# One streaming-encoder layer on one core: the scan's gating on VectorE, a 544-column convolution beside attention, head norm weights after the transposition

## The chip, the core and the metric

The kernel runs on one core of a Trainium2 chip. The core has TensorE (PE in the profile, its weight loads PEld), VectorE (DVE), ScalarE (ACT), GpSimd (POOL) and SyncE (SP, which issues DMAs). The metric is device time in microseconds for one execution, lower is better.

## The reference

One layer of a hybrid encoder on 1024 prompt frames and 64 frames of a running stream, which the kernel treats as T = 1088 columns, all in float32. Cut to what matters here:

```
proj = rmsnorm(x) @ w_in                       # -> z, xBC, dt, q, k, v, gate_ssm, gate_att
xbc  = silu(causal_dwconv(xBC, width 4))       # 3072 channels -> xs, B, C
y    = ssd_scan(xs, dt, B, C) + d * xs         # chunked state-space scan, 4 groups
y    = rmsnorm_per_group(y * silu(z)) * ssm_norm_w
o    = diff_attention(q, k, v, caches, lam)    # 8 heads, two softmaxes each
o    = rmsnorm(o, subln_w) * (1 - lambda_init)
x   += (sig(gate_ssm) * (y @ w_bs) + sig(gate_att) * (o @ w_ba)) @ w_out
x   += conv_ffn(rmsnorm(x))
```

The outputs are the new x, k and v, the scan's end states and the margins of both convolutions.

## The kernel before

Activations are held feature-major: 128 features on the partitions, frames along the columns. Projections multiply 128x128 weight blocks with 272-column quarters (QW) of the activations, two of which make a half (HT = 544). Each float32 product is made of three matmuls of split numbers (`hi`, `lo`; lines 170 to 172, from `product`). The program is written as generators that hand each other turns; from these the tile framework draws up a fixed order of instructions for each engine. A sequencer takes its engine's instructions strictly in that order and waits on semaphores, so an instruction that waits holds up all that stands behind it on its engine.

Two stages matter here.

**Attention** (about 560 to 1130 us of the span). Eight heads with nine query blocks ("units") each. A unit (`attend`) makes scores (L1111, L1112), a maximum (L1116 or L1120 on VectorE), exponentials (L1125 on ScalarE), the combination of both softmaxes (L1129 on VectorE), transpositions (L1140), their evacuation to `a_t` (L1145 ScalarE, L1147 VectorE), and the product with v (L1160), evacuated by ScalarE (L1161, L1162). Between these, `fill` puts in matmuls of a stream of remaining projections (`stream`), so that TensorE has work while the softmax runs: 24 tiles of the convolved projection (`conv_tiles`) and gate tiles (`gate_tiles`).

`conv_tiles` handles each quarter by itself. The previous quarter's last three columns are copied in front by POOL (L987, L989), ScalarE copies the matmuls' result into `pre` (L990), scales and biases it (L999), VectorE adds three shifted multiples (L1001), ScalarE takes the tanh (L1002), VectorE multiplies (L1003, which makes silu), and SyncE stores the result in `x_sc` (L1004). `pre` has two buffers and `cc` three.

`head_out` ends a head. From sums of squares it makes a factor per query (`rs`); nine VectorE instructions L1178 multiply each 128-query block by its factor and by the norm weights `wsub`, which lie along the columns. TensorE then transposes the blocks (L1186), ScalarE evacuates `hi` (L1189) and VectorE `lo` (L1190).

`head_tiles` issues a head's loads: queries, keys, values, and for the ninth unit cached keys and values (`cached`: `ch_t`, `cl_t`, `cv_t`). `cv_t` has two buffers; the cached loads are issued with the rest, but for head 0, whose loads wait in `later`.

**Scan** (about 1130 to 1500 us). Four groups, each with nine 128-frame chunks in three spans of up to 384 columns: 12 spans. `front` prepares a chunk: transpositions `tr` of the inputs (L1285), `cb` (L1287, L1288), the product `xx` on VectorE (L1294), exponentials (L1297), a causal mask by POOL (L1295) and a product on VectorE (L1298). `back` multiplies: `yi` (L1306), `ye` (L1312), sums on VectorE (L1313, L1314), and the new state from `stp` (L1318), with the old state's decay on POOL (L1323) and the sum on VectorE (L1325). At the end of a span, `gated` adds d * xs (L1332, VectorE), multiplies the 4 x 384 values by z (L1333, POOL), squares them (L1334, ScalarE) and adds up the four blocks in two steps (L1335, L1336, POOL). A chunk later `normed` sums over the partitions with TensorE (`gst`, L1340), makes a reciprocal root with ScalarE and L257, L258 on VectorE, and `scaled` multiplies (L1350) and splits (L1359). The same filler continues with the branch projections, whose weights are split by L155 and L156.

## Time and profile before

| what | value |
|---|---|
| median of 3 runs | 2420.58 us (2420.09 to 2423.67) |
| the profiled execution, its own time | 2425.83 us |
| its span, from the first to the last instruction | 2424.0 us |
| mean granted TensorE clock | 0.997 |
| VectorE busy, 560 to 1130 us | 445.2 us |
| VectorE busy, 1130 to 1500 us | 283.0 us |
| POOL busy, 1130 to 1500 us | 161.4 us |

The profile is one execution. Its page has the busy time of each engine, groups of instructions by source line (`L1333 POOL ... x12 | total, mean` with the idle time before them behind a second bar), and a list of waits. Names such as `y<-y,zin` are output and inputs. `x12` is a count. Windows give busy times for a stretch of the span, and the timeline the instructions in order of time.

### The profile page before, as it was taken

The numbers are of one execution on the slowest core, as the hardware profiler recorded it, in microseconds if no ns is written. First come the engines' busy times: TensorE is split into PE (matmuls) and PEld (weight loads), VectorE is DVE, ScalarE is ACT, GpSimd is POOL, SyncE is SP. The second block draws the span as 40 slices with busy tenths as digits, with TensorE's granted clock in tenths as the row PEclk, the third lists the DMA queues.
The fourth block names the chain that finished last, engine by engine and source line by source line (L and its number), as shares of the span: only waits on it lengthen the run. The fifth ranks groups of instructions, "written<-read, shape, count | busy, mean of one in ns | idle before, by whom it ended". The sixth has DMA issues, their size and how long they took to land.

```text
span 2424.0 us, 49267 instructions
## 1 busy us (share of the span) xinstructions
PE 2379.3 (98%) x18648; PEld 2306.1 (95%) x18648; DVE 1750.6 (72%) x3150; ACT 1217.8 (50%) x2695; POOL 731.4 (30%) x773
## 2 busy tenths in 40 slices
PE   8999999999999999999999999999999999999998
PEld 8999999999999999999888899999999999999998
DVE  4678987646868778884789776656866767677765
ACT  6454454325656666665666564334543334352442
POOL 0032433321101101111444442012254455444444
PEclk9999999999999999999999999999999999999999
DMA  7773868536555544435978955764124424367976
GB/s 240 274 245 129 265 218 303 168 104 205 163 157 153 164 143 135 143 104 180 352 264 267 344 190 186 210 208 142 66 82 157 143 98 160 127 199 200 245 182 105
DMA packets 295087, 449.78 MB, mean 186 GB/s; under 512 B 36601, under 2 KB 188290, under 8 KB 294850
## 3 DMA queue, kind: packets, MB, share of 16 engines
q1 hardware_dynamic: 265506, 387.00, 49.5%
q0 software_dynamic: 11040, 26.34, 5.5%
q10 hardware_dynamic: 18304, 33.30, 3.7%
q8 instruction: 146, 2.39, 0.4%
q14 instruction: 91, 0.75, 0.1%
HBM read 294.03 MB, written 152.50 MB: 184 GB/s over the span
## 4 chain that ended last, share of the span: by engine, by line
PE 44%; DVE 6%; DMA 3%; issue 2%; ACT 1%; POOL 1%; SPq 0%; POOLq 0%; DVEq 0%; ACTq 0%
PE mx L1617 13%; PE mx L1791 6%; PE mm L1617 5%; PE mm L170 2%; PE mm L172 2%; PE mm L171 2%; PE mx L170 2%; PE mm L1791 2%; PE mx L172 2%; PE mx L171 2%; PE yi L1306 1%; PE stp L1318 1%; PE ye L1312 1%; DMA b<-y_sc 1%; DMA m_sc<-b_g 1%
## 5 line engine op out<-in xcount | busy, mean ns | idle before, releaser
L170 PE MATMUL mm<-b,w_hi 128*128 128x272 f32 x1376 | 408.7, 297 | 0.0
L172 PE MATMUL mm<-b,w_lo 128*128 128x272 f32 x1376 | 404.2, 294 | 0.0
L171 PE MATMUL mm<-b,w_hi 128*128 128x272 f32 x1376 | 403.0, 293 | 0.0
L170 PEld LDWEIGHTS mm<-b,w_hi 128*128 128x128 f32 x1376 | 259.5, 189 | 5.7 <-issue 3.4
L171 PEld LDWEIGHTS mm<-b,w_hi 128*128 128x128 f32 x1376 | 259.6, 189 | 4.5 <-issue 3.1
L172 PEld LDWEIGHTS mm<-b,w_lo 128*128 128x128 f32 x1376 | 259.1, 188 | 3.6 <-issue 2.5
L1617 PE MATMUL mx<-m,w_hi 128*128 128x272 f32 x792 | 152.3, 290 | 1.2 <-ACT m L419 1.2
L420 DVE TENSOR_TENSOR wh<-w_f,wh 128x512 fp32r<-128x512 f32 (+1 forms) x156 | 151.6, 973 | 0.7 <-ACT wh L419 0.7
L1001 DVE SCALAR_TENSOR_TENSOR cc<-pre,par,cc 128x272 f32<-128x272 f32 (+1 forms) x288 | 139.6, 488 | 9.8 <-ACT cc L999 7.5
L1617 PE MATMUL mx<-n,wh 128*128 128x272 f32 x1056 | 141.6, 288 | 1.1 <-DVE u L1644 1.1
L1125 ACT ACTIVATE p_t<-sc,mx 128x512 f32<-128x512 f32 (+6 forms) x144 | 106.2, 740 | 67.5 <-DVE mx L1116 37.4
L1617 PEld LDWEIGHTS mx<-n,wh 128*128 128x128 f32 x1056 | 135.7, 188 | 1.3 <-DVE u L1644 1.3
L989 POOL COPY pre<-pre 128x3 f32<-128x3 f32 x72 | 27.7, 385 | 346.3 <-DVE cc L1003 182.1
L563 POOL TENSOR_TENSOR ws<-w_f 128x512 f32<-128x512 f32 (+1 forms) x51 | 69.3, 1360 | 198.2 <-DMA w_f<-in_win_dram 82.0
L1617 PEld LDWEIGHTS mx<-m,w_hi 128*128 128x128 f32 x792 | 124.4, 188 | 1.4 <-ACT m L419 1.4
L170 PE MATMUL mx<-b,w_hi 128*128 128x272 f32 x416 | 122.9, 296 | 2.0 <-ACT w_hi L155 1.5
L172 PE MATMUL mx<-b,w_lo 128*128 128x272 f32 x416 | 121.5, 294 | 0.0
L171 PE MATMUL mx<-b,w_hi 128*128 128x272 f32 x416 | 121.4, 292 | 0.0
L1617 PE MATMUL mx<-m,w_lo 128*128 128x272 f32 x396 | 114.2, 289 | 0.0
L1626 ACT ACTIVATE cc<-pre,par 128x544 f32<-128x544 f32 (+1 forms) x44 | 37.2, 846 | 146.2 <-DVE pre L1661 145.3
L156 DVE TENSOR_TENSOR w_lo<-w_f,w_hi 128x1024 fp32r<-128x1024 f32 (+1 forms) x74 | 92.8, 1256 | 22.5 <-ACT w_hi L155 22.1
L419 ACT CAST wh<-w_f 128x512 fp32r<-128x512 f32 (+1 forms) x156 | 95.2, 613 | 27.0 <-POOL w_f L569 8.3
(463 smaller groups left out, 7311.7 us busy)
## 6 DMA issues: line engine op xcount, KB each, us to landing
w_f<-in_win_dram SPq DMA_DIRECT2D x40, 512.0 KB, 4.3
w_f<-in_wup_dram SPq DMA_DIRECT2D x80, 256.0 KB, 2.9
w_f<-in_win_dram SPq DMA_DIRECT2D x76, 256.0 KB, 3.3
bc<-a_sc SPq DMA_DIRECT2D x32, 512.0 KB, 7.1
b<-y_sc SPq DMA_DIRECT2D x24, 544.0 KB, 8.1
h_sc<-hb SPq DMA_DIRECT2D x44, 272.0 KB, 2.1
ht<-h_sc SPq DMA_DIRECT2D x22, 544.0 KB, 4.7
t_sc<-ht SPq DMA_DIRECT2D x22, 544.0 KB, 2.9
```

The lines of the kernel that those rows point to most:

```text
L156: V.tensor_tensor(out=lo, in0=w, in1=hi, op=ALU.subtract)
L170: PE.matmul(ps, a_hi, b_hi, start=i == 0, stop=False)
L171: PE.matmul(ps, a_hi, b_lo, start=False, stop=False)
L172: PE.matmul(ps, a_lo, b_hi, start=False, stop=i == n - 1)
L419: S.copy(hi, src)
L420: V.tensor_tensor(out=lo, in0=src, in1=hi, op=ALU.subtract)
L563: G.tensor_tensor(out=s1, in0=q21, in1=q22, op=ALU.add)
L1001: V.scalar_tensor_tensor(cc[:, :m], pre[:, i : i + m], cw(i), cc[:, :m], ALU.mult, ALU.add)
L1125: act(p_t[:n, :nk], sc[c][:n, :nk], AF.Exp, bias=mx[:n, c : c + 1], accum_out=dst)
L1617: PE.matmul(ps, w[x][:, c], b[y][:, k], start=start and k == i == 0, stop=k == 3 and i == 2, skip_group_check=not start)
L1626: act(cc[:, :n], pre[h][:, :n], AF.Identity, bias=col(O_FB + f), scale=cw(0))
L1791: PE.matmul(ps, w[y][:, c], b[z][:, k], start=start and k == j == 0, stop=k == n - 1 and j == 2, skip_group_check=not start)
```

## The change

Three edits, which touch no projection.

1. In `gated`, the product with z and the two sums of squares go from POOL to VectorE.
2. In `conv_tiles`, the first quarter of each half is only copied into `pre`; the scaling, the three multiples, the tanh, the product and the store are made once per 544-column half. `cc` goes from three buffers to two of twice the width. `cv_t` goes to one buffer, and each head's cached loads are issued with its fourth unit, by way of `later`.
3. In `head_out`, one VectorE product multiplies eight blocks by their factors, and a second instruction the short ninth. The norm weights are applied per partition behind the transposition, in the two evacuations. The column `wcol` comes from one transposition of `wsub` (the tile `pw`) before the first head.

```diff
     def conv_tiles(tiles):
...
+                first = c % HT == 0
+                if first:
+                    pre = cv_pool.tile([P, HT + 6], F32, name="pre", tag="pre", bufs=2)
+                    if tail is None:
+                        G.memset(pre[:, 0:3], 0.0)
+                    else:
+                        G.tensor_copy(pre[:, 0:3], tail)
+                at = 3 + c % HT
                 n = min(w, TP - c)
-                pre = cv_pool.tile([P, QW + 6], F32, name="pre", tag="pre", bufs=2)
-                cc = cv_pool.tile([P, QW + 3], F32, name="cc", tag="cc", bufs=3)
...
+                S.copy(pre[:, at : at + n], ps[:, :n])
...
+                if first:
+                    return
+                c -= QW
+                n, m = min(HT, TP - c), HT
...
+                cc = cv_pool.tile([P, HT + 3], F32, name="cc", tag="cc", bufs=2)
...
-            cv_t = ak.tile([P, 4, P], F32, name="cv_t", tag="cv_t", bufs=2)
+            cv_t = ak.tile([P, 4, P], F32, name="cv_t", tag="cv_t")
...
-                cached()
+            later.append(cached)
...
-            for i in range(9):
-                n = min(P, T - i * P)
-                V.scalar_tensor_tensor(o_t[:n, i], o_t[:n, i], rs[:n, i : i + 1], wsub[:n], ALU.mult, ALU.mult)
+            V.tensor_tensor(out=o_t[:, :8], in0=o_t[:, :8], in1=rs[:, :8].unsqueeze(2).to_broadcast([P, 8, P]), op=ALU.mult)
+            V.tensor_scalar(o_t[:TS, 8], o_t[:TS, 8], rs[:TS, 8:9], None, ALU.mult)
...
-                S.copy(hi, pt[:, :w])
-                V.tensor_tensor(out=lo, in0=pt[:, :w], in1=hi, op=ALU.subtract)
+                act(hi, pt[:, :w], AF.Copy, scale=wcol)
+                V.scalar_tensor_tensor(lo, pt[:, :w], wcol, hi, ALU.mult, ALU.subtract)
...
+        pw = pa.tile([P, 512], F32, name="pw", tag="pt", bufs=2)
+        PE.transpose(pw[:, :P], wsub, ident)
+        S.copy(wcol, pw[:, 0:1])
...
+                if x == 3 and later:
+                    later.pop()()
...
         def gated(g, c, w, xs, zt, y):
...
-            G.tensor_tensor(out=y, in0=y, in1=zt, op=ALU.mult)
+            V.tensor_tensor(out=y, in0=y, in1=zt, op=ALU.mult)
             act(zt, y, AF.Square)
-            G.tensor_tensor(out=zt[:, 0:2], in0=zt[:, 0:2], in1=zt[:, 2:4], op=ALU.add)
-            G.tensor_tensor(out=zt[:, 0], in0=zt[:, 0], in1=zt[:, 1], op=ALU.add)
+            V.tensor_tensor(out=zt[:, 0:2], in0=zt[:, 0:2], in1=zt[:, 2:4], op=ALU.add)
+            V.tensor_tensor(out=zt[:, 0], in0=zt[:, 0], in1=zt[:, 1], op=ALU.add)
```

The framework orders the instructions anew, so both stages' orders differ in many places. Line numbers of the changed kernel are a little higher: L1294, L1298, L1313, L1314, L1325, L1332, L1350 become L1306, L1310, L1325, L1326, L1337, L1344, L1362 (12 more, POOL's L1295 and L1323 become L1307 and L1335), and L1001 and L1003 become L1009 and L1011.

VectorE at the end of the scan's first span, before:

```order
L1294 TENSOR_TENSOR xx<-tr,dtt 128x1024
L1332 SCALAR_TENSOR_TENSOR y<-in,par,y 128x384 x4
L1313 TENSOR_TENSOR y<-ye,e_14870 128x4x128
L1325 TENSOR_TENSOR state<-state,stp 128x512
L1314 TENSOR_TENSOR y<-y,yi 128x4x128
L1294 TENSOR_TENSOR xx<-tr,dtt 128x1024
L1313 TENSOR_TENSOR y<-ye,e_15022 128x4x128
L1325 TENSOR_TENSOR state<-state,stp 128x512
L1298 TENSOR_TENSOR bc<-bc,b_cb 128x1024
```

And now:

```order
L1306 TENSOR_TENSOR xx<-tr,dtt 128x1024
L1344 SCALAR_TENSOR_TENSOR y<-in,par,y 128x384 x4
L1325 TENSOR_TENSOR y<-ye,e_14338 128x4x128
L1337 TENSOR_TENSOR state<-state,stp 128x512
L1345 TENSOR_TENSOR y<-y,zin 128x1536
L1326 TENSOR_TENSOR y<-y,yi 128x4x128
L1306 TENSOR_TENSOR xx<-tr,dtt 128x1024
L1310 TENSOR_TENSOR bc<-bc,b_cb 128x1024
L1325 TENSOR_TENSOR y<-ye,e_14490 128x4x128
L1347 TENSOR_TENSOR zin<-zin 128x768
L1337 TENSOR_TENSOR state<-state,stp 128x512
L1310 TENSOR_TENSOR bc<-bc,b_cb 128x1024
```

The product L1345 stands in front of the next chunk's `y` and `xx`, and the first sum L1347, which waits for ScalarE's square of the product, in front of a state and a `bc`.

POOL at the same place, before:

```order
L1295 AFFINE_SELECT bc<-bc 128x1024
L1323 TENSOR_TENSOR state<-state,decs 128x512
L1333 TENSOR_TENSOR y<-y,zin 128x1536
L1323 TENSOR_TENSOR state<-state,decs 128x512
L1295 AFFINE_SELECT bc<-bc 128x1024
L1335 TENSOR_TENSOR zin<-zin 128x768
L1323 TENSOR_TENSOR state<-state,decs 128x512
L1336 TENSOR_TENSOR zin<-zin 128x384
```

And now:

```order
L1307 AFFINE_SELECT bc<-bc 128x1024
L1335 TENSOR_TENSOR state<-state,decs 128x512 x2
L1307 AFFINE_SELECT bc<-bc 128x1024
L1335 TENSOR_TENSOR state<-state,decs 128x512
L1307 AFFINE_SELECT bc<-bc 128x1024
```

Masks and decays follow each other with nothing between them.

VectorE early in the attention's third head, where `ors` are the factors of the second head, before:

```order
L1175 SCALAR_TENSOR_TENSOR ors<-on_9066,on_9065 128x9
L1178 SCALAR_TENSOR_TENSOR o_t<-o_t,ors,wsub 128x128 x4
L1127 RECIPROCAL sm<-sm 128x1
L1178 SCALAR_TENSOR_TENSOR o_t<-o_t,ors,wsub 128x128 x4
L1178 SCALAR_TENSOR_TENSOR o_t<-o_t,ors,wsub 64x128
L1119 MEMSET sc 64x2x64
L1128 SCALAR_TENSOR_TENSOR sm<-sm,nlam,s_8932 128x1
L1001 SCALAR_TENSOR_TENSOR cc<-pre,par,cc 128x272
L1120 TENSOR_REDUCE mx<-sc 128x2
L1129 SCALAR_TENSOR_TENSOR p_t<-p_t,sm 128x1024
L1001 SCALAR_TENSOR_TENSOR cc<-pre,par,cc 128x272
```

And now:

```order
L1009 SCALAR_TENSOR_TENSOR cc<-pre,par,cc 128x544
L1135 SCALAR_TENSOR_TENSOR sm<-sm,nlam,s_8796 128x1
L1182 SCALAR_TENSOR_TENSOR ors<-on_8922,on_8921 128x9
L1009 SCALAR_TENSOR_TENSOR cc<-pre,par,cc 128x544
L1136 SCALAR_TENSOR_TENSOR p_t<-p_t,sm 128x128
L1183 TENSOR_TENSOR o_t<-o_t,ors 128x1024
L1184 TENSOR_SCALAR o_t<-o_t,ors 64x128
L1154 COPY a_t<-pt 128x512
L1011 SCALAR_TENSOR_TENSOR cc<-pre,cc 128x544
```

Nine instructions on `o_t` have become two, and the wide steps of the convolution stand between the steps of a softmax (`sm`, `p_t`) as the narrow ones did.

More of the change, by code (lines that the diff above doesn't have):

```diff
@@ L978, in conv_tiles @@
         for f in tiles:
[L979 removed]
+            tail = pre = None
             def evac(ps, c, w):
[L982 to L995 removed]
+                nonlocal tail, pre
+                first = c % HT == 0
[6 more added lines that the diff above has]
+                at = 3 + c % HT
+                n = min(w, TP - c)
+                S.copy(pre[:, at : at + n], ps[:, :n])
+                if n < w:
+                    G.tensor_copy(pre[:, at + n : at + n + 3], par[:, O_CS + 3 * f : O_CS + 3 * f + 3])
+                    S.copy(pre[:, at + n + 3 : at + w + 3], ps[:, n:])
+                if first:
+                    return
+                c -= QW
+                n, m = min(HT, TP - c), HT
+                tail = pre[:, n : n + 3]
+                if n < HT:
+                    m = HT + 3
                     G.tensor_copy(conv_o[:, f, 0:3], tail)
[L997 removed]
+                    G.tensor_copy(conv_o[:, f, 3:6], pre[:, HT + 3 : HT + 6])
+                cc = cv_pool.tile([P, HT + 3], F32, name="cc", tag="cc", bufs=2)
                 cw = lambda i: col(O_CW + 4 * f + i)
@@ L1004, in evac @@
                 seen["stored"] = load(out=x_sc[P * f : P * (f + 1), c : c + n], in_=cc[:, :n])
-                if n < w:
-                    load(out=x_sc[P * f : P * (f + 1), c + n : c + w], in_=cc[:, n + 3 : m])
+                if n < HT:
+                    load(out=x_sc[P * f : P * (f + 1), c + n : c + HT], in_=cc[:, n + 3 : m])
             yield from project(win[B_X + f], evac)
@@ L1075, in head_tiles @@
                 values_of()
-                later.append(cached)
             else:
@@ L1202, in hybrid_layer @@
         wsub = at.tile([P, P], F32, name="wsub")
+        wcol = at.tile([P, 1], F32, name="wcol")
         V.tensor_scalar_mul(wsub, par[:, O_SUB : O_SUB + P], 1.0 - LAMBDA_INIT)
+        pw = pa.tile([P, 512], F32, name="pw", tag="pt", bufs=2)
+        PE.transpose(pw[:, :P], wsub, ident)
+        S.copy(wcol, pw[:, 0:1])
         for i in range(2):
```

12 lines of the change are left out of this document (removed).

## The prediction, as it was made before the run

> **What bounds the kernel now.** I read the page's engine totals first, then the two stages that the change touches, then TensorE's own waits there.
>
> ```profile
> PE 2379.3 (98%) x18648; PEld 2306.1 (95%) x18648; DVE 1750.6 (72%) x3150; ACT 1217.8 (50%) x2695; POOL 731.4 (30%) x773
> ```
>
> ```profile
> 560.00:1130.00 570.00, 567.24 (x4351) 543.81 (x4350) 445.24 (x1076) 359.03 (x974) 69.58 (x168) 1.00 0.49 149
> 1130.00:1500.00 370.00, 361.09 (x2912) 323.26 (x2911) 282.97 (x353) 223.86 (x536) 161.37 (x104) 1.00 0.81 268
> 1200.00:1300.00 100.00, 96.71 (x798) 86.77 (x798) 88.07 (x117) 63.52 (x150) 45.11 (x29) 1.00 0.82 273
> ```
>
> In the window rows the columns are length, busy time of PE, PEld, DVE, ACT and POOL, the clock, the DMA share and GB/s. TensorE is busy for 2379.3 of 2424.0 us and the change leaves its work alone except for one transposition. So the change can only move the time by TensorE's waits. In the attention stage (560 to 1130 us) TensorE sits idle for 570 - 567.2 = 2.8 us; in the scan (1130 to 1500) for 370 - 361.1 = 8.9 us. What ends those waits:
>
> ```profile
> PE yi L1306 <- DVE y L1314: 3.1, 2, 1.6
> PE tr L1285 <- DVE xx L1294: 2.3, 3, 1.4
> PE stp L1318 <- DVE state L1325: 1.0, 2, 0.8
> PE yi L1306 <- ACT y L1316: 0.7, 1, 0.7
> PE cb L1287 <- ACT b_cb L1290: 0.6, 1, 0.6
> PE mx L170 <- ACT grs L1343: 0.5, 1, 0.5
> PE gst L1340 <- POOL zin L1336: 0.5, 1, 0.5
> ```
>
> ```profile
> PE sc L1111 <- ACT p_t L1125: 1.1, 1, 1.1
> PE po L1160 <- ACT a_t L1145: 0.9, 2, 0.6
> PE po L1160 <- DVE a_t L1147: 0.5, 1, 0.5
> PE sc L1111 <- DMA kl<-k_st: 0.2, 1, 0.2
> ```
>
> Each row gives the waiter, whom it waited for, total us, times, longest. The scan's rows add up to 8.7 us, of which 6.4 end on VectorE; the attention's to 2.7 us. Those 11.4 us are about all there is to win: 0.5% of the kernel.
>
> **The change part by part: the scan.** Three operations per span (12 spans) leave POOL, which keeps the mask L1295 and the state's decay L1323:
>
> ```profile
> L1333 POOL TENSOR_TENSOR y<-y,zin 128x1536 f32<-128x1536 f32 (+1 forms) x12 | 41.7, 3476 | 35.8 <-DVE y L1332 35.8
> L1335 POOL TENSOR_TENSOR zin<-zin 128x768 f32<-128x768 f32 (+1 forms) x12 | 21.4, 1786 | 10.2 <-ACT zin L1334 10.1
> L1336 POOL TENSOR_TENSOR zin<-zin 128x384 f32<-128x384 f32 (+1 forms) x12 | 16.6, 1380 | 0.6
> L1295 POOL TENSOR_SCALAR_AFFINE_SELECT bc<-bc 128x1024 f32<-128x1024 f32 (+1 forms) x36 | 40.9, 1136 | 132.5 <-ACT e L1282 123.8 <-DMA b<-y_sc 5.4 <-DMA out_dram<-state 3.1
> ```
>
> The numbers behind the bar are total us and mean ns. POOL loses 41.7 + 21.4 + 16.6 = 79.7 us. VectorE takes them over; its prices come from operations of the same kind there (min/median/max ns):
>
> ```profile
> L1298 DVE TENSOR_TENSOR bc<-bc,b_cb x36: 672/1218/3589, 1143.2 to 1468.4; 128x1024 f32<-128x1024 f32 x32, 64x512 f32<-64x512 f32 x4
> L1359 DVE TENSOR_TENSOR y<-y,zin x12: 819/946/1658, 1200.9 to 1329.2; 128x768 fp32r<-128x768 f32 x8, 128x640 fp32r<-128x640 f32 x4
> L258 DVE SCALAR_TENSOR_TENSOR grs<-gn,gn x12: 493/928/1998, 1195.6 to 1498.4; 128x384 f32<-128x384 f32 x8, 128x320 f32<-128x320 f32 x4
> L1350 DVE SCALAR_TENSOR_TENSOR y<-y,par,grs x48: 537/607/3830, 1198.0 to 1500.4; 128x384 f32<-128x384 f32 x32, 128x320 f32<-128x320 f32 x16
> ```
>
> L1298 (1024 columns, two SBUF inputs) has its median at 1218; L1359 gives 946 for 768 columns (its median) and 819 for 640 (its minimum). That is (1218 - 946) / 256 = 1.06 ns a column. The product then takes 1218 + 512 x 1.06 = 1761 ns for 1536 columns and 1218 + 256 x 1.06 = 1489 for 1280; the first sum 946 and 819; the second 946 - 384 x 1.06 = 539 and 819 - 320 x 1.06 = 480. Eight wide and four narrow spans: 8 x 3.25 + 4 x 2.79 = 37.2 us more work on VectorE.
>
> But POOL's operations already cost VectorE time. Two places of the timeline (start, us, engine, line; waits in brackets):
>
> ```profile
> 1285.98 3.49 POOL L1333 TENSOR_TENSOR y<-y,zin 128x1536 f32<-128x1536 f32 x1 [3.08 <-DVE y L1332]
> 1286.43 3.59 DVE L1298 TENSOR_TENSOR bc<-bc,b_cb 64x512 f32<-64x512 f32 x1
> 1291.89 0.33 PE L1306 MATMUL yi<-bc,xx 128*64 128x128 f32 x2 [1.64 <-DVE y L1314]
> ...
> 1365.12 5.81 DVE L1350 SCALAR_TENSOR_TENSOR y<-y,par,grs 128x384 f32<-128x384 f32 x4
> 1365.28 3.78 POOL L1333 TENSOR_TENSOR y<-y,zin 128x1536 f32<-128x1536 f32 x1 [2.62 <-DVE y L1332]
> 1372.12 0.63 PE L1285 MATMUL tr<-con,in 128*64 128x128 f32 x4 [1.45 <-DVE xx L1294]
> ```
>
> A 64x512 product L1298, whose minimum is 672 ns, took 3.59 us and ended with POOL's product L1333, and TensorE's yi then waited 1.64 us. Four L1350, 4 x 607 ns by the median, took 5.81 us beside another L1333, and tr waited 1.45 us. So VectorE operations with two SBUF inputs stand still while POOL computes; L258's maximum of 1998 ns is such a hit too. How much that is over the scan, by the means:
>
> ```profile
> L1298 DVE TENSOR_TENSOR bc<-bc,b_cb 128x1024 f32<-128x1024 f32 x32 | 48.4, 1511 | 20.2 <-ACT bc L1297 11.5 <-ACT b_cb L1290 8.6
> L1350 DVE SCALAR_TENSOR_TENSOR y<-y,par,grs 128x384 f32<-128x384 f32 x32 | 25.0, 842 | 0.2
> ```
>
> L1298: 32 x (1511 - 1218) = 9.4 us; L1350: 32 x (842 - 607) = 7.5. The same difference over all two-input lines of the scan gives 38 us of stretch. By their share of POOL's busy time (79.7 of 161.4) the three leaving operations cause 19 us of it, by their share without the one-input mask (79.7 of 161.4 - 40.9) 25 us. VectorE's net load thus rises by 37.2 - 25 = 12 to 37.2 - 19 = 18 us on 283.0. I take 12, since the two quoted hits are both L1333's.
>
> [...]
>
> On TensorE's path: the two quoted waits go (1.64 + 1.45); gst no longer waits for POOL (0.5); stp's longest wait of 0.8 goes, if L258's stretch was its cause; of the other yi wait (3.1 - 1.64) I give half, 0.7. That is 5.1 us. Added: VectorE now passes 6.4 / 283 = 2.3% of its busy time on to TensorE, so 37.2 us of new work bring 0.9 us of new waits. Bounds of the scan: from 8.7 gained (all waits gone) to 12 lost (rival below). I take 5.1 - 0.9 = **4.2 us gained**.
>
> The new VectorE sums wait for ScalarE's square; queued behind them are xx, state and y, for which TensorE waits. In the order three to five VectorE operations stand between product and first sum, which cover about the square's time, except at the last span, where nothing else is left to hold up.
>
> **The attention.** Wide operations replace pairs of narrow ones; the FFN's convolution has them at 544 columns:
>
> ```profile
> L1001 DVE SCALAR_TENSOR_TENSOR cc<-pre,par,cc x288: 411/494/509, 566.9 to 1107.8; 128x272 f32<-128x272 f32 x120, 128x275 f32<-128x275 f32 x24
> L1003 DVE SCALAR_TENSOR_TENSOR cc<-pre,cc x96: 411/434/446, 570.4 to 1108.9; 128x272 f32<-128x272 f32 x72, 128x275 f32<-128x275 f32 x24
> L999 ACT ACTIVATE cc<-pre,par x96: 599/615/645, 566.2 to 1105.3; 128x272 f32<-128x272 f32 x72, 128x275 f32<-128x275 f32 x24
> L1002 ACT ACTIVATE pre<-cc x96: 414/431/468, 569.6 to 1108.5; 128x272 f32<-128x272 f32 x72, 128x275 f32<-128x275 f32 x24
> L1628 DVE SCALAR_TENSOR_TENSOR cc<-pre,par,cc x88: 773/786/1884, 1729.8 to 2188.9; 128x544 f32<-128x544 f32 x44, 128x546 f32<-128x546 f32 x44
> L1626 ACT ACTIVATE cc<-pre,par x44: 840/846/853, 1724.5 to 2179.6; 128x544 f32<-128x544 f32 x22, 128x546 f32<-128x546 f32 x22
> L1629 ACT ACTIVATE cc<-cc x44: 654/661/667, 1738.0 to 2190.7; 128x544 f32<-128x544 f32 x22, 128x546 f32<-128x546 f32 x22
> L1178 DVE SCALAR_TENSOR_TENSOR o_t<-o_t,ors,wsub x72: 332/343/373, 651.9 to 1126.2; 128x128 f32<-128x128 f32 x64, 64x128 f32<-64x128 f32 x8
> L1129 DVE SCALAR_TENSOR_TENSOR p_t<-p_t,sm x72: 326/809/1289, 580.6 to 1100.2; 128x512 f32<-128x512 f32 x8, 128x128 f32<-128x128 f32 x8, 128x384 f32<-128x384 f32 x8, 128x256 f32<-128x256 f32 x8
> ```
>
> VectorE: L1001 288 x 494 = 142 us becomes 144 x 786 = 113; L1003 96 x 434 = 41.7 becomes 48 operations between 661 and 786 ns (the lower is ScalarE's), say 725: 34.8. The heads' 72 x 343 = 24.7 us become eight 1024-column products of 1.22 us and eight small ones of about 0.34: 12.5. Together 48 us less on 445. ScalarE: L999 96 x 615 = 59.0 becomes 48 x 846 = 40.6; L1002 96 x 431 = 41.4 becomes 48 x 661 = 31.7: 28 us less on 359. The scale put into head_out's two evacuations counts as nothing: the same elements, 24 pairs of instructions; 0.1 us on each would be 5 us off TensorE's path. POOL's copies of the margin halve; POOL is idle for most of the stage. Stores of x_sc halve in number, which shortens SyncE's queue. The wait that changes is ScalarE's copy into pre: a buffer is now held through two quarters and a chain of 0.85 + 3 x 0.79 + 0.73 + 0.66 = 4.6 us. The 96 convolution quarters and 32 gate quarters of these 570 us come every 4.5 us, so the next use of a buffer is over 13 us after its chain begins. Were it late, the softmax's exponentials would queue behind the copy, and TensorE's scores behind them. The cached keys' loads go behind the fourth unit, and are first needed by the ninth; cv_t with one buffer is free by then, as its last reader is the ninth unit of the head before. Nothing of this is on TensorE's path: of its 2.7 us of waits, 2.5 end on ScalarE or VectorE. I take half of these, **1.3 us gained**; bounds 2.7 gained to 10.5 lost (rival below).
>
> The one new transposition stands ahead of the first score, where TensorE already waited 0.2 us for keys: 0 to 0.3 us, I take **0.1 lost**.
>
> Sum: -4.2 - 1.3 + 0.1 = -5.4. The profiled execution took 2425.8 us, 1.8 of it around the span of 2424.0; it would become 2420.4. It lies 5.2 us above the median of the runs, so the forecast there is 2420.6 - 5.4 = **2415.2 us**, 0.22% faster. About 0.2%, 4.8 us, is what a measurement of this kernel can tell from no change.
>
> **The rivals.**
> *More goes than I count.* All 11.4 us of waits vanish: 2409.2. For it: TensorE's waits sit mostly on ScalarE and VectorE, both relieved. Against it: several scan waits (ACT y, ACT b_cb, ACT grs) have nothing to do with POOL.
>
> *The gain is swallowed.* The waits removed come back behind VectorE's own 37 us, or the stretch stays because POOL's mask and decay now hit the new operations: what is left is the attention's 1.3 and little more, 2419. For it: of 38 us of stretch, 13 to 19 belong to operations that stay.
>
> *VectorE becomes the bound in the scan* (the other side). From 1200 to 1300 us VectorE is already busy 88.1 of 100. Twelve spans in 370 us make 3.2 in 100, at 3.1 us each 10.1: 98.2 of 100 if none of the stretch goes. Then 12.3 us, the net load, lie on TensorE's path and none of its waits go: 2420.6 + 12.3 = 2432.9. It decides once VectorE is busy for over some 95% of such a window. Against it: the quoted hits are long, and they go with L1333.
>
> *Wide convolutions hold up the attention.* A softmax step L1129 (72 units) that falls behind a wide operation waits up to 786 - 494 = 292 ns longer, on average half; if TensorE had no cover, 72 x 0.146 = 10.5 us: 2420.6 - 4.2 + 10.5 = 2426.9. Against it: TensorE's queue holds projection matmuls between the units, and waits only 2.8 us now. [...]
>
> **How the numbers follow.** Forecast 0.40, all waits gone 0.08 (both faster by over 0.2%: 0.48); swallowed 0.30 (within); VectorE bound 0.14, wide convolutions 0.08 (slower: 0.22). The range runs from 2407, a little under the second case, to 2430, which takes in the wide convolutions and most of the way to the bound VectorE; about 0.15 lies outside.
>
> **What would show it.** Right: in the scan L1298, L1350 and L258 (now L1310, L1362, L258) keep near their medians with no maximum above 2.5 us; the product L1345 takes 1.5 to 1.8 us; TensorE waits for under 5 us there, and none for POOL; VectorE is busy for about 295 us in those 370, and near 400 in the attention. Wrong: TensorE's waits for xx, y or state grow although the stretch is gone; or new waits for a_t or p_t behind wide operations; or VectorE waiting for the square with TensorE behind it.

## The result, and the profile after

| kernel | median | runs |
|---|---|---|
| before | 2421.47 us (2420.09 to 2424.81) | 6 |
| after | 2413.01 us (2408.63 to 2415.61) | 6 |

The ratio is 0.9962, 95% interval 0.9949 to 0.9975: 6 to 12 us faster, 9 by the middle, where 5.4 were forecast. The profiled execution of the changed kernel took 2411.51 us (span 2409.7), 14.3 less than the one of before. That is more than the runs give: its part up to the first score, ahead of nearly all that the edits touch, is already 2.0 us shorter.

TensorE's waits in the scan of the changed kernel (waiter, whom it waited for, total us, times, longest):

```profile
PE yi L1318 <- ACT y L1328: 1.9, 1, 1.9
PE tr L1297 <- DMA in<-x_sc: 0.7, 1, 0.7
PE yi L1318 <- DVE y L1326: 0.6, 1, 0.6
PE mx L170 <- ACT grs L1355: 0.3, 1, 0.3
```

and in its attention:

```profile
PE pw L1212 <- DMA q<-q_st: 0.6, 1, 0.6
PE sc L1118 <- ACT p_t L1132: 0.5, 1, 0.5
```

The scan's waits add up to 3.5 us where there were 8.7. Those on VectorE fell from 6.4 to 0.6, and none ends on POOL. In the attention 1.1 us are left of 2.7. The two stages in windows (length, busy time of PE, PEld, DVE, ACT, POOL; clock, DMA share, GB/s):

```profile
560.00:1130.00 570.00, 568.81 (x4370) 545.77 (x4369) 419.36 (x829) 342.91 (x881) 43.17 (x120) 1.00 0.48 151
1130.00:1500.00 370.00, 366.50 (x2973) 330.71 (x2972) 301.54 (x393) 229.04 (x541) 90.78 (x68) 1.00 0.81 274
```

In these windows VectorE is busy for 18.6 us more in the scan (301.5) and 25.9 less in the attention (419.4). But the changed scan begins and ends earlier, so that its window takes in more of the next stage: from the first `tr` to the last `gst` VectorE is busy for 294.1 us after 280.5, which is 13.6 more. The lines that had the long hits before, and the new product, with min/median/max in ns:

```profile
L1310 DVE TENSOR_TENSOR bc<-bc,b_cb x36: 672/1214/1920, 1136.3 to 1456.7; 128x1024 f32<-128x1024 f32 x32, 64x512 f32<-64x512 f32 x4
L1362 DVE SCALAR_TENSOR_TENSOR y<-y,par,grs x48: 539/607/2093, 1184.2 to 1488.3; 128x384 f32<-128x384 f32 x32, 128x320 f32<-128x320 f32 x16
L258 DVE SCALAR_TENSOR_TENSOR grs<-gn,gn x12: 475/558/1444, 1179.3 to 1486.3; 128x384 f32<-128x384 f32 x8, 128x320 f32<-128x320 f32 x4
L1345 DVE TENSOR_TENSOR y<-y,zin x12: 1477/1745/2215, 1156.8 to 1472.4; 128x1536 f32<-128x1536 f32 x8, 128x1280 f32<-128x1280 f32 x4
```

L1310 (L1298 before) had a maximum of 3589, L1362 (L1350) 3830, L258 1998. All three are now at or under 2.1 us. The medians of L1310 and L1362 are where they were; L258's fell from 928 to 558.

From the first `tr` to the last `gst` the scan takes 359.6 us after 366.0; from the first score to the first `tr` the attention takes 557.7 after 561.8 (starts of these matmuls in the two timelines). Which instructions TensorE does in each stage shifted a little: counted in the two programs, 13 filler matmuls of about 0.12 us left the attention, and 11 came into the scan.

### The profile page after: what moved, and what is told of

The parts are those of the page before. It is cut to its first block, busy times and chain, and to the rows that moved or that the text cites. A ratio compares the mean times of both kernels' runs of the same rounds, so it can differ in the third digit from the quotient of the medians.

```text
span 2409.7 us, 48636 instructions
## 1 busy us (share of the span) xinstructions
PE 2373.4 (98%) x18649; PEld 2302.2 (96%) x18649; DVE 1729.4 (72%) x2938; ACT 1201.2 (50%) x2600; POOL 634.4 (26%) x689
## 5 line engine op out<-in xcount | busy, mean ns | idle before, releaser
L1009 DVE SCALAR_TENSOR_TENSOR cc<-pre,par,cc 128x544 f32<-128x544 f32 (+1 forms) x144 | 111.2, 772 | 8.2 <-ACT cc L1007 6.9
L1638 ACT ACTIVATE cc<-pre,par 128x544 f32<-128x544 f32 (+1 forms) x44 | 37.2, 846 | 150.0 <-DVE pre L1673 149.1
L155 ACT CAST w_hi<-w_f 128x1024 fp32r<-128x1024 f32 (+1 forms) x74 | 77.6, 1049 | 56.1 <-PE mm L171 30.3
```

The costliest lines, as they stand in the source:

```text
L155: S.copy(hi, w)
L1009: V.scalar_tensor_tensor(cc[:, :m], pre[:, i : i + m], cw(i), cc[:, :m], ALU.mult, ALU.add)
```

## The experiments

All were timed in turns with the kernel before on the same chip; a ratio is to that kernel. There were three sets on three chips, in which the kernel before had medians of 2421.9 us (e1 to e4), 2424.4 (e5, e6, e8, e9) and 2424.8 (e7, e10 to e12), so across sets ratios are compared, and not medians. Two theories stand against each other. **Reading**: POOL's operations that read SBUF hold up VectorE's two-input operations, and TensorE waits for those. **Occupation**: POOL was merely busy, so that its mask and its decay came late; or the edits just drew up another order.

### Each edit by itself

```diff
 # e1: before, with the gating only
-            G.tensor_tensor(out=y, in0=y, in1=zt, op=ALU.mult)
+            V.tensor_tensor(out=y, in0=y, in1=zt, op=ALU.mult)
...
-            G.tensor_tensor(out=zt[:, 0:2], in0=zt[:, 0:2], in1=zt[:, 2:4], op=ALU.add)
+            V.tensor_tensor(out=zt[:, 0:2], in0=zt[:, 0:2], in1=zt[:, 2:4], op=ALU.add)
```

(and the second sum likewise).

> Only the scan's three operations go to VectorE; convolution, head_out and loads as before. Theory (the gain is made where POOL's products stood in VectorE's way): 5 to 8 us faster than before, with the spans between the first tr and the last gst shorter by about 6.5 us and the attention as long as before. Rival (the gain is mostly a matter of relieving VectorE and ScalarE in the attention): under 3 us faster. Rival (VectorE bound in the scan, hidden in the whole by the attention's gain): slower than before.

The second is `conv_tiles` of the change, with the single `cv_t` and the later cached loads, whose room it needs:

```diff
 # e2: before, with the convolution and the cached loads
-                pre = cv_pool.tile([P, QW + 6], F32, name="pre", tag="pre", bufs=2)
+                    pre = cv_pool.tile([P, HT + 6], F32, name="pre", tag="pre", bufs=2)
...
-            cv_t = ak.tile([P, 4, P], F32, name="cv_t", tag="cv_t", bufs=2)
+            cv_t = ak.tile([P, 4, P], F32, name="cv_t", tag="cv_t")
...
```

> Only the convolution 544 columns wide, with the one-buffered cv_t and the later cached loads that make room for it. Theory: the attention's gain of some 4 us is mostly this, so 2 to 4 us faster than before, scan unchanged. Rival (the head norm carries the attention's gain): within 1 us of before. Rival (wide operations hold up the softmax): slower by 2 us or more, with TensorE's waits for a_t or p_t up.

```diff
 # e3: before, with the head's norm only
-            for i in range(9):
-                n = min(P, T - i * P)
-                V.scalar_tensor_tensor(o_t[:n, i], o_t[:n, i], rs[:n, i : i + 1], wsub[:n], ALU.mult, ALU.mult)
+            V.tensor_tensor(out=o_t[:, :8], in0=o_t[:, :8], in1=rs[:, :8].unsqueeze(2).to_broadcast([P, 8, P]), op=ALU.mult)
+            V.tensor_scalar(o_t[:TS, 8], o_t[:TS, 8], rs[:TS, 8:9], None, ALU.mult)
...
```

(with `wcol` and the evacuations of the change).

> Only the norm weights behind the transposition, with the one product for eight blocks. Theory: VectorE loses 12 us of work in 570, TensorE waits little for it, so 0 to 1.5 us faster. Rival (the head norm carries the attention's gain): 3 us or more faster.

```diff
 # e4: before, with the cached loads only
-            cv_t = ak.tile([P, 4, P], F32, name="cv_t", tag="cv_t", bufs=2)
+            cv_t = ak.tile([P, 4, P], F32, name="cv_t", tag="cv_t")
...
-                cached()
+            later.append(cached)
...
+                if x == 3 and later:
+                    later.pop()()
```

> Only the loads of the cached keys and values with the fourth unit and cv_t with one buffer. Theory: no part of the gain, within 1 us of before. Rival (SyncE's queue, freed of waits for the old head's scores, brings weights earlier): 2 us or more faster.

| kernel | median us | ratio (95%) |
|---|---|---|
| e1, gating | 2417.77 | 0.9986 (0.9976 to 0.9995) |
| e2, convolution | 2432.67 | 1.0049 (1.0032 to 1.0066) |
| e3, heads' norm | 2423.76 | 1.0006 (0.9996 to 1.0016) |
| e4, cached loads | 2421.09 | 1.0000 (0.9989 to 1.0012) |

The gating alone is 1 to 6 us faster by its interval, where 5 to 8 were expected, and its scan is 3.3 us shorter (362.7), where 6.5 were expected. Heads' norm and cached loads can't be told from no change. The first three make up the change (e4 is a part of e2), and the four add up to 1.0041, about 10 us slower; together the edits are 9 us faster. **The edits don't add.** The convolution alone is 12 us slower, where 2 to 4 us of gain were expected, and not in the attention, which took 558.3 us after 561.8: it lost 15.5 us in the scan, which it doesn't touch. TensorE's three longest sorts of wait in e2's scan, and the window 1290 to 1310 us:

```profile
PE yi L1315 <- DVE y L1323: 3.5, 1, 3.5
PE mx L172 <- DVE w_lo L156: 3.4, 1, 3.4
PE tr L1294 <- DMA in<-x_sc: 2.4, 1, 2.4
```

```profile
1290.00:1310.00 20.00, 14.04 (x70) 10.30 (x70) 13.98 (x12) 11.57 (x27) 9.37 (x8) 0.57 0.48 165
```

The clock column reads 0.57. By windows of 1 us it was at 0.50 for 17.1 us from 1292 on, right behind TensorE's waits for `in` (2.4 us) and for y (3.5 us). e1 had the like in small: 4.3 us waiting for `grs`, and then 3.4 us at half clock.

```profile
PE cb L1287 <- ACT grs L1343: 4.3, 1, 4.3
PE tr L1285 <- DMA in<-x_sc: 2.7, 3, 1.5
```

### Without one of the edits

```diff
 # e5: the changed kernel, gating left on POOL
-            V.tensor_tensor(out=y, in0=y, in1=zt, op=ALU.mult)
+            G.tensor_tensor(out=y, in0=y, in1=zt, op=ALU.mult)
...
-            V.tensor_tensor(out=zt[:, 0:2], in0=zt[:, 0:2], in1=zt[:, 2:4], op=ALU.add)
-            V.tensor_tensor(out=zt[:, 0], in0=zt[:, 0], in1=zt[:, 1], op=ALU.add)
+            G.tensor_tensor(out=zt[:, 0:2], in0=zt[:, 0:2], in1=zt[:, 2:4], op=ALU.add)
+            G.tensor_tensor(out=zt[:, 0], in0=zt[:, 0], in1=zt[:, 1], op=ALU.add)
```

> The whole change but for the scan: convolution, loads and head norm changed, the product with z and its sums left on POOL. The convolution alone was 11 us slower than before, all of it lost in the scan, the whole change 9 us faster. Theory (in the scan, POOL's products stall VectorE, and how much that costs TensorE depends on where the order puts them; with the sums on VectorE there is nothing left to collide): slower than the whole change by 10 to 22 us, so between 1 and 12 us slower than before, with VectorE's operations stretched to 3.5 us beside the product, and TensorE's waits in the scan over 8 us. Rival (the convolution's loss needs the old head norm, and the norm edit mends it): within 4 us of the whole change.

e6 is the changed kernel with `head_out` of before (the minus lines of e3's diff).

> The whole change but for the head norm: scan, convolution and loads changed. Theory: as fast as the whole change within 2 us (7 to 10 us faster than before), since the norm alone changed nothing and the convolution's loss is in the scan, where the scan's edit takes away its cause. Rival (the norm edit is needed for the gain): under 4 us faster than before, or slower.

```diff
 # e7: the changed kernel, the two sums left on POOL
-            V.tensor_tensor(out=zt[:, 0:2], in0=zt[:, 0:2], in1=zt[:, 2:4], op=ALU.add)
-            V.tensor_tensor(out=zt[:, 0], in0=zt[:, 0], in1=zt[:, 1], op=ALU.add)
+            G.tensor_tensor(out=zt[:, 0:2], in0=zt[:, 0:2], in1=zt[:, 2:4], op=ALU.add)
+            G.tensor_tensor(out=zt[:, 0], in0=zt[:, 0], in1=zt[:, 1], op=ALU.add)
```

> The whole change, but the two sums of squares stay on POOL; only the product with z goes to VectorE. Theory (the products on POOL did the harm, since their reads hold up VectorE): nearly all of the gain stays, 0 to 3 us above the changed kernel, ratio to before 0.996 to 0.998. Rival (every reading of POOL counts by its time: the sums were 38 of 79.7 us): half the gain is lost, about 2418, ratio 0.998 to 1.000. Second rival (VectorE's load counts): faster than the changed kernel, since VectorE is relieved of 18 us.

| kernel | median us | ratio (95%) |
|---|---|---|
| e5, no gating | 2430.54 | 1.0030 (1.0020 to 1.0040) |
| e6, no heads' norm | 2414.31 | 0.9960 (0.9947 to 0.9973) |
| e7, sums on POOL | 2426.62 | 1.0015 (1.0006 to 1.0024) |

The heads' norm is worth nothing that can be measured. The gating is worth 16 us beside the wide convolution (ratios 1.0030 and 0.9962), though 3 beside the narrow one. And e7 refutes all that I expected of it: with the product on VectorE and only the sums on POOL the whole gain is gone. e5's and then e7's main waits in the scan:

```profile
PE tr L1297 <- DVE xx L1306: 4.7, 1, 4.7
PE tr L1297 <- DMA in<-x_sc: 3.8, 1, 3.8
PE yi L1318 <- DVE y L1326: 3.2, 2, 2.2
PE gst L1352 <- POOL zin L1348: 0.8, 1, 0.8
```

```profile
PE gst L1352 <- POOL zin L1348: 2.8, 2, 1.6
PE mx L172 <- DVE w_lo L156: 2.4, 1, 2.4
PE tr L1297 <- DMA in<-x_sc: 1.9, 1, 1.9
```

In e5 VectorE is held up as the prediction had it, and more than in the kernel before. From its timeline (start, us, engine; the wait in brackets):

```profile
1176.57 3.78 POOL L1345 TENSOR_TENSOR y<-y,zin 128x1536 f32<-128x1536 f32 x1
1176.94 4.50 DVE L1310 TENSOR_TENSOR bc<-bc,b_cb 128x1024 f32<-128x1024 f32 x1
1182.39 4.50 DVE L1362 SCALAR_TENSOR_TENSOR y<-y,par,grs 128x384 f32<-128x384 f32 x4
1188.07 1.06 PE L1297 MATMUL tr<-con,in 128*64 128x128 f32 x4 [4.68 <-DVE xx L1306]
```

L1310, 1.2 us by the median, takes 4.5 beside POOL's product; the four L1362, 4 x 0.61, take 4.5 beside POOL's sums; `xx` stands behind them, and TensorE waits 4.7 us for it. At 1285 us a 64x512 L1310, 0.67 us at the least, takes 7.6 while POOL does six operations in a row, and the wait of 2.2 us for `y` is behind that one. e2 has the same at the same places (L1359 beside the sums, then 3.4 us of waiting for `w_lo`; L1307 with 7.6 us, then 3.5 for `y`).

In e7, with the product gone from POOL, no operation of VectorE takes over 1.5 us more than the median of its kind in the scan; in e5 ten do, in the kernel before six. There it is two of POOL's operations that take long:

```profile
1185.43 4.26 POOL L1347 TENSOR_TENSOR zin<-zin 128x768 f32<-128x768 f32 x1 [1.69 <-ACT zin L1346]
1189.77 4.29 POOL L1348 TENSOR_TENSOR zin<-zin 128x384 f32<-128x384 f32 x1
```

By their medians in e7 these two sums take 1.8 and 1.5 us; `gst` waits 1.2 us for the second.

In both kernels `gst` waits for POOL's sums, and `tr` waits for a load of `in`. That load is the one for the first span of the third group, the seventh of the twelve spans. `in` has two buffers, so the load waits until the span before last has done its d * xs (L1344), the last reader. The three events in e7 and then in the changed kernel (start, us, engine; SPq is SyncE's queue, L1272 the load's last part):

```profile
1280.20 2.98 DVE L1344 SCALAR_TENSOR_TENSOR y<-in,par,y 128x384 f32<-128x384 f32 x4
1284.26 0.43 SPq L1272 DMA_DIRECT2D in<-x_sc  x1
1291.75 0.63 PE L1297 MATMUL tr<-con,in 128*128 128x128 f32 x4 [1.92 <-DMA in<-x_sc]
```

```profile
1274.93 2.19 DVE L1344 SCALAR_TENSOR_TENSOR y<-in,par,y 128x384 f32<-128x384 f32 x4
1277.99 1.16 SPq L1272 DMA_DIRECT2D in<-x_sc  x1
1286.71 0.60 PE L1297 MATMUL tr<-con,in 128*128 128x128 f32 x4
```

In the changed kernel TensorE comes to the transposition 11.8 us after d * xs has begun, and the load has landed. In e7 the four d * xs begin 5.3 us later, are stretched from 2.19 to 2.98 us, and TensorE is there 9.6 us after (1291.75 - 1.92 - 1280.20). The same distance in the other profiles, with the wait: e5 8.4 (3.8 us), e2 8.5 (2.4), e10 below 10.0 (3.0), e6 10.6 (1.5); e12 11.3, before 11.7 and after 11.8 without a wait. In e1 11.9 were not enough (1.0), and at the eleventh span of before 10.2 were, so some 10 to 12 us are needed: for d * xs, for SyncE's queue and for the load, which in e7 landed 7.5 us after its last part was issued. e6 and e10 have all of the gating on VectorE and come too near nevertheless. Behind e7's wait the clock drops:

```profile
1290.00:1310.00 20.00, 18.25 (x94) 15.10 (x95) 10.72 (x15) 13.91 (x34) 5.78 (x6) 0.66 0.67 205
```

It is at half speed for 13.6 us from 1292 on; the `ye` there take 421 ns by the median, and 275 at full clock. The wait with the clock behind it makes 8.7 of the 16.6 us by which e7's scan is longer than the changed kernel's, and in e5 at most 7.2 of 18.8; most of the rest are the waits for VectorE and POOL above, behind which another 3.4 us run at half clock in each (from 1187 us on).

**One account for all.** For each profile: the scan's length, TensorE's waits in it, and the time lost to the clock (the sum of 1 minus the granted clock over windows of 1 us).

| kernel | scan us | waits | lost to the clock | remainder |
|---|---|---|---|---|
| before | 366.0 | 8.2 | 0.0 | 357.8 |
| after | 359.6 | 3.2 | 0.0 | 356.4 |
| e1 | 362.7 | 7.7 | 1.7 | 353.3 |
| e2 | 381.5 | 16.0 | 10.2 | 355.3 |
| e5 | 378.4 | 17.3 | 5.1 | 356.0 |
| e6 | 362.1 | 5.6 | 0.0 | 356.5 |
| e7 | 376.2 | 10.3 | 8.5 | 357.4 |

The remainder stays between 353 and 358 while the scan varies by 22 us (the other kernels: 354 to 359, and 361 in e3, with 33 filler matmuls more). So what sets these scans apart is TensorE's waits, 3.2 to 17.3 us in the table, and the time lost to the clock, 0 to 10.2.

### Reading or occupation

Useless work was put on POOL in the changed kernel; its result is read by nobody. In e8 and e9 it isn't tied to anything, and all of it ran early, within 77 and 64 us of the first `tr`.

```diff
 # e8 (e9: six times G.memset(dead, 0.0))
...
+            for _ in range(3):
+                G.tensor_tensor(out=dead, in0=con[:, :448], in1=con[:, :448], op=ALU.mult)
             V.tensor_tensor(out=y, in0=y, in1=zt, op=ALU.mult)
```

> The changed kernel with useless work for POOL in the scan: for each span three products of two SBUF inputs, 448 columns each, whose result nobody reads (about 3 us of POOL a span). Theory (POOL's reads stall VectorE's two-input operations): VectorE's stretch in the scan comes back, 10 us or more above that of the changed kernel, and 3 to 8 us of the gain are lost. Rival (the gain comes from the shorter chain from product to gst, which stays as short here): within 1.5 us of the changed kernel, so 7 us or more faster than before.

> As the kernel with useless products, but POOL fills a tile with zeros instead, six times 448 columns for each span: POOL is kept from its masks and decays in the same places, and reads nothing. Theory (it is the reading): no stretch of VectorE's operations, within 1.5 us of the changed kernel. Rival (masks and decays queued behind POOL's work are what costs time): as slow as the kernel with useless products.

e8: 2424.11 us, ratio 1.0000 (0.9989 to 1.0010). e9: 2419.72, ratio 0.9985 (0.9975 to 0.9995). Neither is as expected: all of the gain is lost in e8, and e9, to be within 1.5 us of the changed kernel, is 5.6 slower by its ratio. From the first `tr` to the fourth `gst` (the second span's), where the useless work lies, the changed kernel takes 76.5 us, e8 83.8 and e9 77.5. Reading costs 7 us there and writing 1. But e9 lost 6 us more later on, where POOL had no useless work left (a load of `in` was 2.4 us late at 1378 us, and behind a wait of 2.1 us at 1521 the clock halved), so these two don't settle it. e11 and e12 pin the same work behind each span's d * xs, where the old product stood:

```diff
 # e11 (e12: six times G.memset(dead, 0.0))
+            flag = sp.tile([P, 1], F32, name="flag", tag="flag", bufs=2)
+            V.tensor_copy(out=flag, in_=y[:, 3, :1])
+            behind = G.tensor_copy(out=dead[:, :1], in_=flag)
+            with tc.issue_after(behind.ins):
+                for _ in range(3):
+                    G.tensor_tensor(out=dead, in0=con[:, :448], in1=con[:, :448], op=ALU.mult)
             V.tensor_tensor(out=y, in0=y, in1=zt, op=ALU.mult)
```

> The changed kernel plus useless work on POOL, which nothing reads: three products of 448 columns with two SBUF inputs behind each span's last d * xs, where the old product stood (about 36 us in all, beside a flag copy per span that pins them). Theory (reading on POOL holds up VectorE): VectorE's operations beside them are stretched by 8 to 15 us and the time rises by 3 to 10 us over the changed kernel, ratio to before 0.998 to 1.001. Rival (POOL's being late for the mask and the decay was the harm): the time rises as in the memset kernel, and the stretch beside the useless work stays under 2 us.

> As the kernel with useless reading, but with six memsets of 448 columns at the same places, which occupy POOL for about as long (34 us) and read nothing. Theory (reading holds up VectorE): within 2 us of the changed kernel, stretch beside the memsets under 2 us. Rival (an occupied POOL makes mask and decay late): as much slower as the kernel with useless reading, with TensorE's waits ending on bc or state.

e11: 2418.24 us, ratio 0.9974 (0.9963 to 0.9984). e12: 2411.89, ratio 0.9951 (0.9936 to 0.9965), the same as the changed kernel. The scan's window in e11, then in e12:

```profile
1130.00:1500.00 370.00, 363.60 (x2944) 326.87 (x2943) 311.43 (x405) 228.44 (x541) 143.41 (x116) 1.00 0.82 271
```

```profile
1130.00:1500.00 370.00, 367.71 (x2983) 331.92 (x2983) 297.21 (x405) 230.95 (x543) 132.76 (x152) 1.00 0.83 275
```

VectorE does the same work in both, but is busy for 311.4 us beside reading and 297.2 beside writing; from the first `tr` to the last `gst` it is 304.6 and 288.6, with 396 instructions in each. Two of its lines show where, first in e11, then in e12 (L1370 is L1362 of the changed kernel):

```profile
L1310 DVE TENSOR_TENSOR bc<-bc,b_cb 128x1024 f32<-128x1024 f32 x32 | 42.0, 1312 | 10.1 <-ACT b_cb L1302 7.0 <-ACT bc L1309 3.0
L1310 DVE TENSOR_TENSOR bc<-bc,b_cb 64x512 f32<-64x512 f32 x4 | 4.4, 1098 | 0.0
L1370 DVE SCALAR_TENSOR_TENSOR y<-y,par,grs 128x384 f32<-128x384 f32 x32 | 22.7, 769 | 0.1
```

```profile
L1310 DVE TENSOR_TENSOR bc<-bc,b_cb 128x1024 f32<-128x1024 f32 x32 | 39.5, 1233 | 8.0 <-ACT bc L1309 4.6 <-ACT b_cb L1302 3.4
L1310 DVE TENSOR_TENSOR bc<-bc,b_cb 64x512 f32<-64x512 f32 x4 | 2.7, 675 | 0.0
L1370 DVE SCALAR_TENSOR_TENSOR y<-y,par,grs 128x384 f32<-128x384 f32 x32 | 20.4, 700 | 0.1
```

The 64x512 product L1310 takes 1098 ns on the mean beside reading and 675 beside writing. POOL's useless work in e11, then in e12:

```profile
L1352 POOL TENSOR_TENSOR dead<-con 128x448 f32<-128x448 f32 x36 | 44.0, 1223 | 2.5
L1352 POOL MEMSET dead<- 128x448 f32 x72 | 34.0, 472 | 3.8
```

So reading did the stretching, and occupying POOL for 34 us costs nothing that shows. The two kernels' scans are 4.9 us apart (363.1 and 358.2), 3.9 of it TensorE's waits (5.7 and 1.8). In the medians they are 6.3 us apart; the intervals of their ratios touch, but five of e12's six runs are faster than each of e11's eight. Against the changed kernel, whose interval e11's overlaps, a loss isn't shown, and e11's ratio lies below the expected 0.998 to 1.001.

That it is operations with both inputs in SBUF which are longer shows in VectorE's other lines. Those with one input in PSUM, where TensorE writes, have the same means in e11 and e12 to within 4 ns: `xx` L1306 1217 and 1218 ns, L1337 676 and 680, and with 512 columns L1325 681 and 684 and L1326 681 in both. In the profile of before these lines (there L1294, L1325, L1313 and L1314), beside POOL or not, have maxima of 1225, 689, 693 and 689 ns with medians of 1217, 679, 682 and 679. Of the lines with both inputs in SBUF most are longer in e11, as the product L1353, 2032 and 1750 ns for 1536 columns; L1379 isn't, 1048 and 1116 for 768.

### All that reads leaves POOL

```diff
 # e10: the changed kernel, the state's decay on VectorE too
-                G.tensor_tensor(out=new.rearrange("p (e q) -> p e q", e=8)
+                V.tensor_tensor(out=new.rearrange("p (e q) -> p e q", e=8)
```

(with its other operands as they were).

> The changed kernel with the state's decay on VectorE too, so that POOL keeps only the mask in the scan. Theory (a two-input reading on POOL holds up VectorE): VectorE gets 32 operations of 0.68 us, 22 us, and loses the 11 us of stretch beside the decay; TensorE's waits of 3.5 us change little: 0 to 3 us slower than the changed kernel. Rival (VectorE is near its bound in the scan): the 11 us net come out on TensorE's path, 8 to 12 us slower, with windows of 20 us in which VectorE is busy for 19.5 or more. If both are wrong and the stretch is worth more than it measures, it is faster than the changed kernel by 1 to 3 us.

2413.61 us, ratio 0.9956 (0.9942 to 0.9970): the same as the changed kernel, as expected, though the 32 decays are 24.8 us of work on VectorE; it is busy for 11.2 us more (305.3 from the first `tr` to the last `gst`), so the rest was stretch that went. But for 0.3 us for `grs`, no wait for VectorE or ScalarE is left among TensorE's in the scan, only loads that are late, with the clock behind them:

```profile
PE tr L1297 <- DMA in<-x_sc: 3.3, 2, 3.0
```

```profile
1290.00:1310.00 20.00, 16.99 (x92) 14.07 (x87) 12.06 (x20) 11.84 (x28) 2.18 (x2) 0.66 0.70 219
```

d * xs comes at 1281.84 here, the load's last part is issued at 1287.76, and `tr` starts at 1294.81. Of the scan's 364.8 us, 3.6 are waits and 6.8 lost to the clock; the remainder is 354.4. This execution (2416.78 us) was the slowest of the five, so not each lost as much. Whether an earlier load would turn this into a gain wasn't tried.

## Why the prediction was right, and where not

**What bounds.** That only TensorE's waits can be won held: the remainder in the table hardly moves. What it left out is the clock: e2's scan lost 10.2 us to it beside 16.0 us of waits and e7's 8.5 beside 10.3, so that the risk was larger than the prize of 11.4 us.

**The scan, 4.2 us forecast.** TensorE's waits fell by 5.0 us in the traces (8.2 to 3.2), and the scan by 6.4, though it holds 11 filler matmuls more. The two quoted hits went, as forecast, and the wait for ScalarE's y grew from 0.7 to 1.9 us, where 0.9 in all was allowed for. The prices were right:

```profile
L1345 DVE TENSOR_TENSOR y<-y,zin 128x1536 f32<-128x1536 f32 (+1 forms) x12 | 20.7, 1728 | 0.1
L1347 DVE TENSOR_TENSOR zin<-zin 128x768 f32<-128x768 f32 (+1 forms) x12 | 11.3, 938 | 4.0 <-ACT zin L1346 4.0
L1348 DVE TENSOR_TENSOR zin<-zin 128x384 f32<-128x384 f32 (+1 forms) x12 | 8.4, 702 | 0.1
```

That is 20.7, 11.3 and 8.4 us, 40.4 in all, where 37.2 was worked out; the second sum is the dear one, at 702 ns for 539. The first sum's wait did hold up what is queued behind it: in the first span VectorE stood idle for 0.93 us until 1163.02, when the square was there, though the state L1337, next in its order, had its inputs at 1159.53 (L1335) and 1161.43 (`stp`); it began behind the sum, at 1163.89. But none of TensorE's waits in the changed kernel's scan ends on the state. The net load on VectorE came to 13.6 us from the first `tr` to the last `gst`, where 12 was taken: 26.8 of the 40.4 us were made up for by stretch that went, where 25 was taken. Most of that was the product's, as assumed: in e7, where the product alone has moved, VectorE is busy for 283.4 us, 2.9 more than before for 19.9 of new work. That reading is what stretches is shown by e11 and e12. POOL's operations grew longer in turn: its 68 masks and decays took 91.1 us after 82.9, 8 us more. The decay L1335 at 1156.98 us took 2.55 us, with VectorE's product L1345 beside it from 1156.77 to 1158.62; by the median the decay takes 1.05. But none of TensorE's waits ends there.

**The step that failed is the sum of the edits**: each was priced against the waits of before, as if the order beside it stayed. The measured terms are -3.4 for the gating alone (2421.9 x 0.0014), +11.9 for the convolution alone (0.0049), and -9.2 for all. With such terms, that the whole came out near the forecast is in part luck. The wide convolution leaves another order of the scan. With the gating on POOL (e2, e5) VectorE is held up in that order where TensorE waits for it, and d * xs comes too short ahead of the seventh span's transposition. So the forecast's mechanism, POOL's reading holds up VectorE and TensorE waits for that, was right, but its price belongs to the order that the edits make together: 16 us there, 3 in the order of before. It isn't all of the account either: in e7 VectorE is free of such hits and the gain is gone all the same, by late sums on POOL, a late load and the clock. Why the wide convolution's order brings d * xs and the transposition so close, and whether in e7 the late sums or just the order do so, wasn't traced further.

**The attention, 1.3 us forecast.** It took 4.1 us less, 1.6 of it for the 13 filler matmuls that moved out, so 2.5; its waits fell by 1.6. The heads' norm, a quarter of VectorE's relief there as forecast, shows no effect on the time (e6). VectorE's busy time fell by 25.9 us and not by 48. Its lines before and after:

```profile
L1001 DVE SCALAR_TENSOR_TENSOR cc<-pre,par,cc 128x272 f32<-128x272 f32 (+1 forms) x288 | 139.6, 488 | 9.8 <-ACT cc L999 7.5
L1003 DVE SCALAR_TENSOR_TENSOR cc<-pre,cc 128x272 f32<-128x272 f32 x96 | 41.5, 432 | 7.9 <-ACT pre L1002 7.7
L1178 DVE SCALAR_TENSOR_TENSOR o_t<-o_t,ors,wsub 128x128 f32<-128x128 f32 (+1 forms) x72 | 19.7, 342 | 0.2
```

```profile
L1009 DVE SCALAR_TENSOR_TENSOR cc<-pre,par,cc 128x544 f32<-128x544 f32 (+1 forms) x144 | 111.2, 772 | 8.2 <-ACT cc L1007 6.9 <-issue 0.2
L1011 DVE SCALAR_TENSOR_TENSOR cc<-pre,cc 128x544 f32<-128x544 f32 (+1 forms) x48 | 34.3, 715 | 5.2 <-ACT pre L1010 5.2
L1183 DVE TENSOR_TENSOR o_t<-o_t,ors 128x1024 f32<-128x1024 f32 x8 | 9.8, 1225 | 0.2
```

By count times mean it is 29.4 + 7.2 + 14.8 less, 2.2 more for the short ninth block, and 1.5 more for the evacuation L1196, whose factor was costed at nothing: 47.7, as forecast. All durations of VectorE from the first score to the first `tr` say the same: 447.6 us after 495.1, 47.5 less, but busy time fell by 26.8 there (415.8 after 442.6). What failed is to take durations for busy time. In the records an instruction mostly starts some 0.07 to 0.085 us ahead of the end of the one before; durations count that time twice and busy time once. With 249 instructions fewer this is the other 20.7 us, which never were VectorE's. `L1178` shows it in one row: 72 x 342 ns is 24.6, its busy time 19.7.

**The transposition `pw`, 0.1 forecast**: 0.6 us of wait, for the load of queries.

**The rivals.** *VectorE as the bound*: after the change it is busy for 91.6 of the 100 us from 1200 on, not for that rival's 98.2, and e10 put 11 us net on it and lost nothing. The 95% at which the rival was to decide was its author's estimate; no run shows such a point. *Wide convolutions hold up the attention*: e2 is slower by about what that rival priced, 11.9 us for 10.5, but its attention is 3.5 us shorter; the size is right by luck, the place wrong. *Swallowed*: e11 comes nearest, where POOL keeps reading.

**The signs.** Maxima under 2.5 us, a scan with under 5 us of waits, none for POOL, VectorE near 295 (301.5): as said. The product took 1477 to 2215 ns, 1745 by the median, for 1.5 to 1.8 us. VectorE in the attention, 419 for 400, was not.

## What to carry to other kernels

Price a set of edits together, against the order that they make together: here one that costs 12 us alone belonged to a whole that gains 9. Look for a late release: a double-buffered load that hangs on the last reader of the span before last turned delays on VectorE into waits of TensorE of 1.9 us (e7, where d * xs came 5.3 us later) and up to 3.8 us (e5). And look at the clock around TensorE's long waits: in these scans 12 of 13 waits of over 1.9 us lay in a stretch of 3.4 to 17.1 us at half clock, or up to 8 us ahead of one.

## What the chip showed that I had not expected

The half clock came in steps of 3.4 us: the scans have stretches of 3.4 (e1, e2, e5, e7), 6.8 (e5), 13.6 to 13.7 (e7, e10) and 17.1 us (e2). In the scans of all profiles, 12 of 13 waits of over 1.9 us lie in such a stretch or up to 8 us ahead of it; e9's of 2.4 us doesn't, and neither does the changed kernel's of 1.89. No shorter wait there has one behind it by itself. Elsewhere shorter waits have one in some profiles and not in others: near 2190 us all fourteen profiles have the same wait of 1.49 to 1.55 us for `u`, and the clock halved behind it in nine and not in five. Near 1715 us two waits of about 1 us in a row did it in seven of them. The kernel before has two such drops in its profile, behind idle times of 1.5 and 1.9 us at 2191.6 and 2266.1, each 3.4 us at half clock and a window with 0.89 x 15 us:

```profile
2185.00:2200.00 15.00, 12.91 (x83) 11.76 (x82) 14.82 (x21) 6.25 (x11) 7.62 (x6) 0.89 0.48 126
2260.00:2275.00 15.00, 13.14 (x92) 12.92 (x92) 15.00 (x19) 10.00 (x14) 5.34 (x6) 0.89 1.11 301
```

They cost that execution 3.4 us which the profiled execution of the changed kernel didn't lose: a part of the 14.3 us between the two profiles, and no effect of the change. In e7 TensorE's records, whose ends are modelled, fill 13 of the 13 us from 1293 to 1306, and the clock stays at half all the same.
